# A transformer layer on one core: wider weight blocks in one feed-forward stage, and another spacing of the modulation rows

## The chip, the core and the metric

The kernel runs on one core of a Trainium2 chip. The metric is the device time of one execution in microseconds (us). Lower is better. The time of the kernel before is the median of 3 runs, 1873.0 us.

The engines are named as in the profile: PE (matrix products; PEld is its weight load, which overlaps them), DVE (vector operations), ACT (activations and casts), POOL, and SP, which here only issues DMAs.

## What is computed

One layer over 256 rows of 2048 numbers, in float32. Nine modulation vectors of 2048 numbers come from a conditioning vector `c`. They shift, scale and gate three sub-layers: feed-forward, token mixer (attention and a recurrent part), feed-forward.

```python
ada = (silu(c) @ w_ada + b_ada)            # 2048 x 18432 weights, one vector in
sh1, sc1, g1, sh2, sc2, g2, sh3, sc3, g3 = split(ada, 9)
h = swiglu(layernorm(x) * (1 + sc1) + sh1, ffn1_w_in, ffn1_w_out)
x = layernorm(ALPHA * x + 0.5 * (1 + g1) * h, ln1_g, ln1_b)
h = token_mixer(layernorm(x) * (1 + sc2) + sh2, w_in, ..., w_out)
x = layernorm(ALPHA * x + (1 + g2) * h, ln2_g, ln2_b)
h = swiglu(layernorm(x) * (1 + sc3) + sh3, ffn2_w_in, ffn2_w_out)
x = layernorm(ALPHA * x + 0.5 * (1 + g3) * h, ln3_g, ln3_b)
# swiglu(h) = (silu(h @ w_gate) * (h @ w_up)) @ w_out, with 5632 hidden columns
```

## The kernel before, in words

**Products.** Each float32 operand is split into a high part and a rest (`hi`, `lo`), and a product is three matmuls of these parts (`mm3`, L420 to L422). A weight block of 1 MB is loaded by SP into one of three places called `raw` (`load_w`). It is then split in two halves: ACT casts `hi` (L155), DVE subtracts to get `lo` (L156). `hi` and `lo` have six places each, so the split can run up to three blocks ahead of PE.

**Stages, in order.** First input, first part (`first_in`, tiles `s`, `raw_s`): half of the first feed-forward's hidden columns, while the first modulation vectors are made. First input, second part (`ffn_in` with tag `f1`, tiles `gu_f`, `raw_f1i`, from about 311 to 526.5 us): the other hidden columns, `j` from 12 to 21. First output (`out_proj` with tag `f1`, `raw_f1o`, to about 757 us). A layer norm (`boundary`). The mixer (783 to 1159 us): `cols_1024`, `cols_form_b`, `form_a_four`, then `out_proj` with tag `mx`. A second layer norm, and the second feed-forward to the end.

**The second part of the first input.** For each `j` and each of gate and up (`gu`), 256 columns are computed from two blocks of 1024 inputs by 256 columns. One PSUM tile of 512 columns holds gate and up of one group of 128 hidden columns. After both, ACT takes the Silu of gate and DVE multiplies (L459, L460).

**The ada rows.** The modulation vectors are not made by PE but by DVE, beside the products. A unit is 1024 columns of `w_ada` over 2048 inputs, in 16 rows of 128 inputs. A row (called an ada row below) is a 512 KB load by SP into one of two places `araw` (L189; `ar` in the profile) and one multiply-add on DVE into an accumulator `acc` or `gate` (L170). After 16 rows a tail splits the sum (`alo`), sums it over partitions on PE (`bc`, L183), and spreads it (`dg`, `scsh`, or into `gate`, L200 to L215).

**What sets their order.** `AdaQueue` holds the units in order. After each weight block a stage calls `pump(rate)`. This adds the rate to a debt, does one step of a pending tail, and issues whole rows while the debt is at least 1. The rates are one line of constants (`R_F`, `R_IN`, `R_OUT`, `R_MX`, ...). A unit of the first stage can't start before the layer norm that follows it allows it (`stage`), and a unit with its own accumulator waits for pending tails that have one. `need(n)` forces what is missing before a point of use, and drops the debt. `finish1` needs 6 units (96 rows) before the first layer norm; the mixer's output needs 10 units.

**Queues.** SP issues its loads in program order and stops at one whose place is still in use. DVE, ACT and PE run in order too. So an ada row whose load is late holds up everything behind it on DVE.

**The mixer's recurrent heads.** For head `h`, PE makes `gb` and `sps` (L1426, L1428), ACT an exponential of `gb`, and DVE multiplies them into `dm` (L1433, L1434). `sps` has one place (`fifth_tile`), so the `sps` of head 1 waits until DVE has read that of head 0.

Of the kernel before, what the change touches and what calls it, by code (L numbers as in the profile page):

```python
# [9 lines left out]
AF = mybir.ActivationFunctionType  # L10
ALU = mybir.AluOpType
# [3 lines left out]
P = 128  # L15
T = 256
D = 2048
KD = D // P
DFF = 5632
# [13 lines left out]
def layer_kernel(  # L33
# [8 lines left out]
    V, S, G_, PE, SP = nc.vector, nc.scalar, nc.gpsimd, nc.tensor, nc.sync  # L42
# [101 lines left out]
    pin = {}  # L144
# [9 lines left out]
    def split(src, hi, lo):  # L154
        S.copy(hi, src)  # L155
        return V.tensor_tensor(out=lo, in0=src, in1=hi.bitcast(F32), op=ALU.subtract)  # L156
# [62 lines left out]
    class AdaQueue:  # L219
# [42 lines left out]
        def pump(self, n):  # L262
            self.owed += n
            self.end_step()
            while self.owed >= 1:
                with pinned():
                    if not self.row():
                        break
                self.owed -= 1
# [104 lines left out]
    def new_xT(tag):  # L374
        x = xp.tile([P, KD, 2, T], F32R, name=f"x_{tag}")
        return x[:, :, 0], x[:, :, 1], x


    def load_w(src, nk, w, name, by_parts=False, behind=None, into=None):
        raw = wp.tile([P, nk, w], F32, tag="raw", bufs=3, name=f"raw_{name}")  # L380
        src = src.rearrange("(k p) n -> p k n", p=P)
        if not by_parts:
            SP.dma_start(raw, src)
        h = nk // 2 if nk * w <= 2048 else nk // 4
        for q in range(nk // h):
            if by_parts:
                SP.dma_start(raw[:, q * h:(q + 1) * h], src[:, q * h:(q + 1) * h])
            if into:
                hi, los = into[q]
                S.copy(hi, raw[:, q * h:(q + 1) * h, :])  # L390
                n = h // len(los)
                for i, lo in enumerate(los):
                    pin["w"] = V.tensor_tensor(out=lo, in0=raw[:, q * h + i * n:q * h + (i + 1) * n, :],
                                               in1=hi[:, i * n:(i + 1) * n, :].bitcast(F32), op=ALU.subtract).ins
                for kk in range(h):
                    yield q * h + kk, hi[:, kk, :], los[kk // n][:, kk % n, :]
                continue
            hi = wp.tile([P, h, w], F32R, tag="hi", bufs=6, name=f"hi_{name}{q}")
            lo = wp.tile([P, h, w], F32R, tag="lo", bufs=6, name=f"lo_{name}{q}")
            with ExitStack() as s:  # L400
                if behind:
                    s.enter_context(tc.issue_after(behind))
                pin["w"] = split(raw[:, q * h:(q + 1) * h, :], hi, lo).ins
            for kk in range(h):
                yield q * h + kk, hi[:, kk, :], lo[:, kk, :]

    def woven(b):
        if b.shape[-1] % 256:
            return b
        return b.rearrange("p (a n) -> p n a", a=2)  # L410

    def unwoven(ps):
        return ps.rearrange("p (n a) -> p a n", a=2)

    def halves(v):
        return v.rearrange("p (a n) -> p a n", a=2)

    def mm3(o, ah, al, bh, bl, start, stop):
        bh, bl = woven(bh), woven(bl)
        PE.matmul(o, ah, bh, start=start, stop=False)  # L420
        PE.matmul(o, ah, bl, start=False, stop=False)  # L421
        PE.matmul(o, al, bh, start=False, stop=stop)  # L422

    def mm2(o, ah, al, x, start, stop):
        PE.matmul(o, ah, x.rearrange("p s (a n) -> p s n a", a=2), start=start, stop=False)  # L425
        PE.matmul(o[:, T:], al, woven(x[:, 0]), start=False, stop=stop)  # L426


    def cols_form_a(src, c0, outs, xT, name, npump, khs=(0, 1)):
        xhi, xlo, x = xT  # L430
        for kh in khs:
            for k8, hi, lo in load_w(src[kh * 1024:(kh + 1) * 1024, c0:c0 + 256], 8, 256, f"{name}_{kh}"):
                k = kh * 8 + k8
                for f in range(2):
                    fs = slice(f * P, (f + 1) * P)
                    start, stop = k == 8 * khs[0], k == 8 * khs[-1] + 7
                    if outs[f].shape[-1] == 2 * T:
                        mm2(outs[f], hi[:, fs], lo[:, fs], x[:, k], start, stop)
                    else:
                        mm3(outs[f], hi[:, fs], lo[:, fs], xhi[:, k, :], xlo[:, k, :], start, stop)  # L440
            npump()

    def ffn_in(w, xT, hT, j0, tag, npump, values=None):
        def one(j, gu, outs):
            last = gu and j == DFF // 256 - 1
            cols_form_a(w, gu * DFF + j * 256, outs, xT, f"{tag}i{j}_{gu}", (lambda: None) if last else npump)

        def both(dst, ps):
            S.copy(dst, unwoven(ps[:, :T]))
            V.tensor_tensor(out=dst, in0=dst, in1=unwoven(ps[:, T:]), op=ALU.add)  # L450

        for j in range(j0, DFF // 256):
            if values is None:
                ps = [mm_tile(f"gu_{tag}{j}_{f}") for f in range(2)]
                for gu in range(2):
                    one(j, gu, [p[:, gu * T:(gu + 1) * T] for p in ps])
                for f in range(2):
                    h = halves(hT[:, 2 * j + f, :])
                    S.activation(h, unwoven(ps[f][:, :T]), AF.Silu)  # L459
                    pin["h"] = V.tensor_tensor(out=h, in0=h, in1=unwoven(ps[f][:, T:]), op=ALU.mult).ins  # L460
                continue
            for gu in range(2):
                ps = [mm_tile(f"gu_{tag}{j}_{gu}{f}") for f in range(2)]
                one(j, gu, ps)
                for f in range(2):
                    h = halves(hT[:, 2 * j + f, :])
                    if gu:
                        u = halves(values.tile([P, T], F32, tag="u", bufs=2, name=f"u_{tag}{j}_{f}"))
                        both(u, ps[f])
                        pin["h"] = V.tensor_tensor(out=h, in0=h, in1=u, op=ALU.mult).ins  # L470
                    else:
                        both(h, ps[f])
                        S.activation(h, h, AF.Silu)
        for _ in range(2):
            npump()

# [311 lines left out]
    def entry_of(load, got, u0, u1):  # L788
        for u in range(u0, u1):
            got[u] = []  # L790
            for item in load(u):
                got[u].append(item)
                yield

    R_F, R_IN, R_OUT, R_MX, R_A, R_B = 1.25, 1.2, 1, 1.42, 1.05, .6
    NP = 2
    right = dict(side="right")
    def at(rate):  # L800
        return lambda: pump(rate)
# [18 lines left out]
    hT = Rows(hp, "hT1")  # L820
# [3 lines left out]
    xT = new_xT("f1")  # L824
    W1 = ffn1_w_in[0]
# [127 lines left out]
    NS = 12  # L953
# [99 lines left out]
    def first_hi_places(tag):  # L1053
        ent["hi0"] = tc.alloc_tile_pool(name=f"hi0{tag}", bufs=1)
        ent["hi"] = [ent["hi0"].tile([P, 2, T], F32R, name=f"hi{tag}_{k}") for k in range(0, 8, 2)]

    first_hi_places("1")
    ffn_in(W1, xT, hT, NS, "f1", at(R_IN))
    xp.release()
    need(2)  # L1060
    W = w_in[0]
# [76 lines left out]
    xhi, xlo, _ = xT  # L1138
# [377 lines left out]
    for i, c0 in enumerate((C_MQ, C_MK)):  # L1516
        ps = form_a_four(c0, f"m{i}")
# [76 lines left out]
    xT = new_xT("f2")  # L1594
# [13 lines left out]
    hT = Rows(hp, "hT2")  # L1608
# [23 lines left out]
    for j in range(2, 10):  # L1632
# [18 lines left out]
    for j in range(2, 10):  # L1651
        for gu, ps in enumerate(half_in(j, 1, "fs")):
# [7 lines left out]
            for f in range(2):  # L1660
                i = 2 * j + f
                h = hT[:, i + 16 * gu, :]
# [55 lines left out]
```

## Time and profile before

| what | value |
|---|---|
| median of 3 runs | 1873.0 us (1867.44 to 1874.89) |
| profiled execution, its own time | 1878.46 us |
| span of the profiled execution | 1876.8 us |
| granted TensorE clock, mean | 0.996 |
| DMA moved | 510.74 MB, mean 272 GB/s |

The span runs from the first to the last instruction; 1.7 us of the profiled execution's own time lie around it. In the views, a row of windows gives for a stretch of time the busy time of each engine with its instruction count, then the granted clock, the mean busy share of the 16 DMA engines and the rate in GB/s. A row of waits names who waited, for whom, how long in total, how often, and the longest. A row of the timeline has start, length, engine, line, operation and tiles, and in square brackets the idle time before it and what ended it.

### The profile page before, as it was taken

The numbers are of one execution on the slowest core, as the hardware profiler recorded it, in microseconds if no ns is written. First come the engines' busy times: TensorE is split into PE (matmuls) and PEld (weight loads), VectorE is DVE, ScalarE is ACT, GpSimd is POOL, SyncE is SP. The second block draws the span as 40 slices with busy tenths as digits, with TensorE's granted clock in tenths as the row PEclk, the third lists the DMA queues.
The fourth block names the chain that finished last, engine by engine and source line by source line (L and its number), as shares of the span: only waits on it lengthen the run. The fifth ranks groups of instructions, "written<-read, shape, count | busy, mean of one in ns | idle before, by whom it ended". The sixth has DMA issues, their size and how long they took to land.

```text
span 1876.8 us, 29775 instructions
## 1 busy us (share of the span) xinstructions
PE 1829.0 (97%) x11881; PEld 1673.8 (89%) x11881; DVE 1465.0 (78%) x1883; ACT 911.8 (49%) x1320; POOL 62.2 (3%) x92
## 2 busy tenths in 40 slices
PE   7999999999999999999989999999999999999997
PEld 5999999999998888699989887888999999988887
DVE  6888989778788886878879788988977766574655
ACT  3554363443454433845556545565444454554441
POOL 1211200000000000100000000000000000000000
PEclk9999999999999999999999999999999999999999
DMA  9988978999998898489978894998878776666664
GB/s 365 383 279 294 333 232 274 313 312 325 296 315 305 309 329 296 136 301 331 316 254 307 303 314 142 307 305 265 271 253 265 260 241 193 201 202 204 205 204 146
DMA packets 283906, 510.74 MB, mean 272 GB/s; under 512 B 10834, under 2 KB 134386, under 8 KB 282744
## 3 DMA queue, kind: packets, MB, share of 16 engines
q1 hardware_dynamic: 275656, 477.90, 75.0%
q0 software_dynamic: 8112, 30.95, 4.8%
q8 instruction: 93, 1.52, 0.3%
q14 instruction: 45, 0.37, 0.1%
HBM read 506.71 MB, written 2.10 MB: 271 GB/s over the span
## 4 chain that ended last, share of the span: by engine, by line
PE 38%; DMA 10%; DVE 8%; issue 2%; ACT 2%; POOL 0%; DVEq 0%; ACTq 0%; SPq 0%; POOLq 0%
PE gu_f L425 9%; DMA ar<-in_w_ada_dram 7%; PE gu_f L426 4%; PE o_f L421 4%; PE o_f L420 4%; PE o_f L422 4%; PE fs L425 3%; DMA raw_fh<-in_ffn_w_in_dram 2%; DVE acc L170 2%; PE fs L426 1%; DVE gate L170 1%; PE fh L425 1%; PE b_mv L421 1%; PE b_mv L420 1%; PE b_mv L422 1%
## 5 line engine op out<-in xcount | busy, mean ns | idle before, releaser
L170 DVE SCALAR_TENSOR_TENSOR acc<-ar,csil,acc 128x1024 f32<-128x1024 f32 (+1 forms) x167 | 211.7, 1269 | 74.3 <-DMA ar<-in_w_ada_dram 73.7
L425 PE MATMUL gu_f<-x_f,hi_f2i 128*128 128x512 f32 x768 | 251.8, 382 | 0.0
L422 PE MATMUL s<-x_f,lo_s 128*128 128x256 f32 x768 | 211.9, 276 | 0.8 <-DVE lo_s L156 0.7
L420 PE MATMUL s<-x_f,hi_s 128*128 128x256 f32 x768 | 212.2, 277 | 0.2 <-ACT x_f L336 0.2
L421 PE MATMUL s<-x_f,hi_s 128*128 128x256 f32 x768 | 212.0, 276 | 0.0
L426 PE MATMUL gu_f<-x_f,lo_f2i 128*128 128x256 f32 x768 | 209.3, 273 | 0.0
L422 PE MATMUL gu_f<-x_f,lo_f1i 128*128 128x256 f32 x640 | 176.4, 276 | 1.4 <-DVE lo_f1i L156 1.3
L421 PE MATMUL gu_f<-x_f,hi_f1i 128*128 128x256 f32 x640 | 176.0, 275 | 0.0
L420 PE MATMUL gu_f<-x_f,hi_f1i 128*128 128x256 f32 x640 | 176.0, 275 | 0.0
L156 DVE TENSOR_TENSOR lo_f2o<-raw_f2o,hi_f2o 128x1024 fp32r<-128x1024 f32 x86 | 105.2, 1225 | 86.9 <-ACT hi_f2o L155 86.8
L156 DVE TENSOR_TENSOR lo_f2i<-raw_f2i,hi_f2i 128x1024 fp32r<-128x1024 f32 x96 | 117.5, 1224 | 65.7 <-ACT hi_f2i L155 64.8
L425 PEld LDWEIGHTS gu_f<-x_f,hi_f2i 128*128 128x128 f32 x768 | 145.1, 189 | 20.3
L155 ACT CAST hi_s<-raw_s 128x1024 fp32r<-128x1024 f32 x96 | 99.5, 1051 | 128.7 <-PE s L421 77.0
L422 PEld LDWEIGHTS s<-x_f,lo_s 128*128 128x128 f32 x768 | 147.9, 193 | 1.2 <-DVE lo_s L156 1.2
L421 PEld LDWEIGHTS s<-x_f,hi_s 128*128 128x128 f32 x768 | 147.9, 193 | 0.4 <-DVE x_f L339 0.4
L420 PEld LDWEIGHTS s<-x_f,hi_s 128*128 128x128 f32 x768 | 147.8, 193 | 0.3 <-ACT x_f L336 0.3
L426 PEld LDWEIGHTS gu_f<-x_f,lo_f2i 128*128 128x128 f32 x768 | 147.4, 192 | 0.2
L155 ACT CAST hi_f2o<-raw_f2o 128x1024 fp32r<-128x1024 f32 x86 | 90.0, 1047 | 115.7 <-PE o_f L422 107.5
L155 ACT CAST hi_f2i<-raw_f2i 128x1024 fp32r<-128x1024 f32 x96 | 100.4, 1045 | 91.3 <-PE gu_f L425 65.3
L155 ACT CAST hi_f1o<-raw_f1o 128x1024 fp32r<-128x1024 f32 x86 | 88.5, 1047 | 113.7 <-DMA raw_f1o<-in_ffn_w_out_dram 55.0
L170 DVE SCALAR_TENSOR_TENSOR gate<-ar,csil,gate 128x1024 f32<-128x1024 f32 (+1 forms) x94 | 117.6, 1252 | 29.0 <-DMA ar<-in_w_ada_dram 28.9
L155 ACT CAST hi_f1i<-raw_f1i 128x1024 fp32r<-128x1024 f32 x80 | 81.3, 1049 | 111.6 <-DMA raw_f1i<-in_ffn_w_in_dram 80.2
(449 smaller groups left out, 5095.4 us busy)
## 6 DMA issues: line engine op xcount, KB each, us to landing
ar<-in_w_ada_dram SPq DMA_DIRECT2D x230, 512.0 KB, 5.5
raw_f2i<-in_ffn_w_in_dram SPq DMA_DIRECT2D x48, 1024.0 KB, 5.2
raw_s<-in_ffn_w_in_dram SPq DMA_DIRECT2D x47, 1024.0 KB, 7.6
raw_f1o<-in_ffn_w_out_dram SPq DMA_DIRECT2D x44, 1024.0 KB, 7.3
raw_f2o<-in_ffn_w_out_dram SPq DMA_DIRECT2D x44, 1024.0 KB, 5.2
raw_f1i<-in_ffn_w_in_dram SPq DMA_DIRECT2D x40, 1024.0 KB, 7.8
ar<-in_w_ada_dram POOLq DMA_DIRECT2D x45, 512.0 KB, 6.4
raw_mxo<-in_w_out_dram SPq DMA_DIRECT2D x16, 1024.0 KB, 7.7
```

The source lines that it names most:

```text
L155: S.copy(hi, src)
L156: return V.tensor_tensor(out=lo, in0=src, in1=hi.bitcast(F32), op=ALU.subtract)
L170: V.scalar_tensor_tensor(out=acc, in0=raw, scalar=csil[:, k:k + 1], in1=acc, op0=ALU.mult, op1=ALU.add)
L420: PE.matmul(o, ah, bh, start=start, stop=False)
L421: PE.matmul(o, ah, bl, start=False, stop=False)
L422: PE.matmul(o, al, bh, start=False, stop=stop)
L425: PE.matmul(o, ah, x.rearrange("p s (a n) -> p s n a", a=2), start=start, stop=False)
L426: PE.matmul(o[:, T:], al, woven(x[:, 0]), start=False, stop=stop)
```

## The change

The second part of the first input gets a function of its own. It takes 512 columns at a time, in blocks of 512 inputs by 512 columns, again 1 MB each: each row of a block is now 2 KB in one piece where it was 1 KB. For each 512 columns it runs four blocks of gate and then four of up. One PSUM tile now holds two groups of 128 columns of gate, or two of up. The Silus of four groups follow each other after the gate blocks, and four multiplies after the up blocks. There are 40 blocks before and after, 1920 matmuls of the same shape, 20 Silus and 20 multiplies of the same shape, and 40 calls of `pump` (two blocks at the end call none, two calls stand behind). The old branch without `values` goes.

Two rates change: `R_IN` from 1.2 to 1.3, `R_MX` from 1.42 to 1.3.

```diff
+    def ffn_in_512(w, xT, hT, q0, tag, npump):
+        xhi, xlo, _ = xT
+        for q in range(q0, DFF // 512):
+            for gu in range(2):
+                ps = [mm_tile(f"gu_{tag}{q}_{gu}{i}") for i in range(2)]
+                for u in range(4):
+                    c0 = gu * DFF + q * 512
+                    for k4, hi, lo in load_w(w[u * 512:(u + 1) * 512, c0:c0 + 512], 4, 512, f"{tag}i{q}_{gu}{u}"):
+                        k = 4 * u + k4
+                        for f in range(4):
+                            fs = slice(f * P, (f + 1) * P)
+                            mm3(ps[f // 2][:, f % 2 * T:(f % 2 + 1) * T], hi[:, fs], lo[:, fs], xhi[:, k, :], xlo[:, k, :],
+                                k + f % 2 == 0, k + f % 2 == KD)
+                    if not (gu and q == DFF // 512 - 1 and u > 1):
+                        npump()
+                for f in range(4):
+                    h, p = halves(hT[:, 4 * q + f, :]), unwoven(ps[f // 2][:, f % 2 * T:(f % 2 + 1) * T])
+                    if gu:
+                        pin["h"] = V.tensor_tensor(out=h, in0=h, in1=p, op=ALU.mult).ins
+                    else:
+                        S.activation(h, p, AF.Silu)
...
-    R_F, R_IN, R_OUT, R_MX, R_A, R_B = 1.25, 1.2, 1, 1.42, 1.05, .6
+    R_F, R_IN, R_OUT, R_MX, R_A, R_B = 1.25, 1.3, 1, 1.3, 1.05, .6
...
-    ffn_in(W1, xT, hT, NS, "f1", at(R_IN))
+    ffn_in_512(W1, xT, hT, NS // 2, "f1", at(R_IN))
```

The rates move ada rows against everything else. In names such as `ar6_0_4`, the first two numbers are the unit and the last is its row, 0 to 15; the number behind is a buffer's.

On SP, at the end of the first output: `raw_f1o1536_5` to `_10` are the last weight blocks of that product, and `raw_mo0` is the first of the mixer. Before:

```order
L383 DMA raw_f1o1536_5_7823<-in_ffn1_w_out_dram 128x4x512
L189 DMA ar6_0_0_8427<-in_w_ada_dram 128x2x512
L383 DMA raw_f1o1536_6_7857<-in_ffn1_w_out_dram 128x4x512
L189 DMA ar6_0_1_8454<-in_w_ada_dram 128x2x512
L383 DMA raw_f1o1536_7_7919<-in_ffn1_w_out_dram 128x4x512
L383 DMA raw_f1o1536_8_7927<-in_ffn1_w_out_dram 128x4x512
L383 DMA raw_f1o1536_9_7944<-in_ffn1_w_out_dram 128x4x512
L383 DMA raw_f1o1536_10_7954<-in_ffn1_w_out_dram 128x4x512
L1066 DMA raw_mo0_8070<-in_w_in_dram 128x2x1024
```

The same place on SP with the change:

```order
L383 DMA raw_f1o1536_8_7956<-in_ffn1_w_out_dram 128x4x512
L189 DMA ar6_0_2_7847<-in_w_ada_dram 128x2x512
L189 DMA ar6_0_3_7850<-in_w_ada_dram 128x2x512
L383 DMA raw_f1o1536_9_7966<-in_ffn1_w_out_dram 128x4x512
L189 DMA ar6_0_4_7853<-in_w_ada_dram 128x2x512
L189 DMA ar6_0_5_7890<-in_w_ada_dram 128x2x512
L383 DMA raw_f1o1536_10_7976<-in_ffn1_w_out_dram 128x4x512
L189 DMA ar6_0_6_7927<-in_w_ada_dram 128x2x512
L1078 DMA raw_mo0_8092<-in_w_in_dram 128x2x1024
```

Before, two rows of unit 6_0 are loaded ahead of the layer norm and none is added up there. With the change rows 0 to 8 of it are loaded and rows 0 to 6 are added up ahead of the layer norm, five of their loads between or behind the last three weight blocks.

On DVE, in the mixer, between the last splits of the block group `fb` and the multiplication of head 0 (`dm0`, which frees `sps0`). Before:

```order
L156 TENSOR_TENSOR lo_fb30_10221<-raw_fb3_10218,hi_fb30_10220 128x1024
L156 TENSOR_TENSOR lo_fb31_10249<-raw_fb3_10218,hi_fb31_10248 128x1024
L170 SCALAR_TENSOR_TENSOR acc5_0_9893<-ar5_0_7_10276,csil_94,acc5_0_9893 128x1024
L170 SCALAR_TENSOR_TENSOR acc5_0_9893<-ar5_0_8_10279,csil_94,acc5_0_9893 128x1024
L200 TENSOR_TENSOR dg6_1_1_10187<-bc6_1_1_10184,ident_79 128x512
L202 TENSOR_REDUCE scsh_103<-dg6_1_1_10187 128x4
L204 TENSOR_TENSOR scsh_103<-scsh_103,bcol_98 128x2x4
L1433 TENSOR_TENSOR dm0_10206<-dm0_10206,trir_87 128x128 x2
L1434 TENSOR_TENSOR dm0_10206<-sps0_10205,dm0_10206 128x256
```

The same place on DVE with the change:

```order
L156 TENSOR_TENSOR lo_fb30_10233<-raw_fb3_10230,hi_fb30_10232 128x1024
L156 TENSOR_TENSOR lo_fb31_10261<-raw_fb3_10230,hi_fb31_10260 128x1024
L170 SCALAR_TENSOR_TENSOR acc5_0_9622<-ar5_0_11_10288,csil_94,acc5_0_9622 128x1024
L1445 TENSOR_TENSOR dm0_10218<-dm0_10218,trir_87 128x128 x2
L1446 TENSOR_TENSOR dm0_10218<-sps0_10217,dm0_10218 128x256
```

One ada row stands ahead of `dm0` where two and the end of a tail stood.

On SP, the loads of these rows among the weight blocks `fb` and `fbk`. Before:

```order
L383 DMA raw_fb3_10218<-in_w_in_dram 128x4x512
L189 DMA ar5_0_6_10191<-in_w_ada_dram 128x1024
L189 DMA ar5_0_7_10276<-in_w_ada_dram 128x1024
L383 DMA raw_fbk0_10298<-in_w_in_dram 128x4x512
L383 DMA raw_fbk1_10390<-in_w_in_dram 128x4x512
L189 DMA ar5_0_8_10279<-in_w_ada_dram 128x1024
```

With the change:

```order
L383 DMA raw_fb3_10230<-in_w_in_dram 128x4x512
L189 DMA ar5_0_9_10134<-in_w_ada_dram 128x1024
L189 DMA ar5_0_10_10203<-in_w_ada_dram 128x1024
L383 DMA raw_fbk0_10307<-in_w_in_dram 128x4x512
L189 DMA ar5_0_11_10288<-in_w_ada_dram 128x1024
L383 DMA raw_fbk1_10402<-in_w_in_dram 128x4x512
```

The last row ahead of `dm0` was behind both blocks `fbk0` and `fbk1` (row 8); it is now behind `fbk0` alone (row 11).

More of the change, by code (lines that the diff above doesn't have):

```diff
@@ L441, in cols_form_a, with ffn_in @@
             npump()
[L443 to L446, printed above, removed]
+    def ffn_in(w, xT, hT, j0, tag, npump, values):
         def both(dst, ps):
@@ L452, in ffn_in @@
         for j in range(j0, DFF // 256):
[L453 to L461, printed above, removed]
             for gu in range(2):
                 ps = [mm_tile(f"gu_{tag}{j}_{gu}{f}") for f in range(2)]
-                one(j, gu, ps)
+                last = gu and j == DFF // 256 - 1
+                cols_form_a(w, gu * DFF + j * 256, ps, xT, f"{tag}i{j}_{gu}", (lambda: None) if last else npump)
                 for f in range(2):
@@ L473, in ffn_in @@
                         S.activation(h, h, AF.Silu)
+        for _ in range(2):
+            npump()
[13 more added lines that the diff above has]
+                    if not (gu and q == DFF // 512 - 1 and u > 1):
+                        npump()
+                for f in range(4):
[4 more added lines that the diff above has]
+                        S.activation(h, p, AF.Silu)
         for _ in range(2):
```

## Prediction

> **What bounds the kernel now.** I read the page first, then the windows by stage, then PE's waits inside the stages that the change touches.
>
> ```profile
> span 1876.8 us, 29775 instructions
> PE 1829.0 (97%) x11881; PEld 1673.8 (89%) x11881; DVE 1465.0 (78%) x1883; ACT 911.8 (49%) x1320; POOL 62.2 (3%) x92
> ```
>
> PE is busy for 1829.0 of 1876.8 us. A change that leaves PE's work alone can only remove idle time, 47.8 us in all, or slow matmuls behind it. The windows show where that idle time lies (columns: length, busy PE, PEld, DVE, ACT, POOL, clock, DMA share, GB/s).
>
> ```profile
> core 0: us, PE busy (x) PEld busy (x) DVE busy (x) ACT busy (x) POOL busy (x), PEclk, DMA share, GB/s
> 311.00:526.50 215.50, 214.09 (x1897) 212.81 (x1896) 166.34 (x170) 89.22 (x108) 1.08 (x2) 1.00 0.94 310
> 526.50:757.00 230.50, 230.50 (x1068) 201.13 (x1067) 189.13 (x209) 102.00 (x119) 2.59 (x3) 1.00 0.86 301
> 783.00:1159.00 376.00, 361.42 (x2438) 335.41 (x2436) 314.28 (x471) 205.03 (x372) 9.30 (x13) 1.00 0.85 293
> ```
>
> The stage that gets the new code (311 to 526.5) has 215.50 - 214.09 = 1.4 us of idle PE, the first output behind it none, the mixer 376.00 - 361.42 = 14.6 us. So the new block shape can win at most 1.4 us where it stands. What can be won lies in the mixer, where the change only moves ada rows. PE's waits there:
>
> ```profile
> PE sps L1428 <- DVE dm L1434: 5.0, 1, 5.0
> PE o_mx L422 <- DVE ylo L156: 2.9, 1, 2.9
> PE o_mx L420 <- ACT yF L1251: 2.1, 1, 2.1
> PE pr_fb L422 <- DVE lo_fb L156: 1.5, 1, 1.5
> PE b_fv L421 <- DVE lo_fv L156: 1.0, 1, 1.0
> PE b_mv L421 <- DVE lo_mv L156: 0.8, 1, 0.8
> ```
>
> Nearly all end with DVE, and one is 5.0 us long. DVE's timeline just before its end tells why:
>
> ```profile
> 943.31 0.69 DVE L156 TENSOR_TENSOR alo<-gate,ahi 128x512 fp32r<-128x512 f32 x1
> 943.91 2.36 DVE L156 TENSOR_TENSOR lo_fb<-raw_fb,hi_fb 128x1024 fp32r<-128x1024 f32 x2
> 946.19 1.28 DVE L170 SCALAR_TENSOR_TENSOR acc<-ar,csil,acc 128x1024 f32<-128x1024 f32 x1
> 952.17 1.28 DVE L170 SCALAR_TENSOR_TENSOR acc<-ar,csil,acc 128x1024 f32<-128x1024 f32 x1 [4.71 <-DMA ar<-in_w_ada_dram]
> 953.38 0.68 DVE L200 TENSOR_TENSOR dg<-bc,ident 128x512 f32<-128x512 f32 x1
> 954.10 0.69 DVE L202 TENSOR_REDUCE scsh<-dg 128x4 f32<-128x512 f32 x1
> 954.82 0.17 DVE L204 TENSOR_TENSOR scsh<-scsh,bcol 128x8 f32<-128x8 f32 x1
> 954.90 0.49 DVE L1433 TENSOR_TENSOR dm<-dm,trir 128x128 f32<-128x128 f32 x2
> 955.30 0.42 DVE L1434 TENSOR_TENSOR dm<-sps,dm 128x256 f32<-128x256 f32 x1
> ```
>
> DVE stands 4.71 us for the load of an ada row (row 8 of unit 5_0). Behind it in order are a tail's last steps (1.5 us) and `dm0`, which frees the only place of `sps`. SP shows why the row is late:
>
> ```profile
> 935.93 5.10 SPq L383 DMA_DIRECT2D raw_fbk<-in_w_in_dram  x2
> 943.43 0.34 SPq L189 DMA_DIRECT2D ar<-in_w_ada_dram  x1
> ```
>
> Its load is issued at 943.43, behind two 1 MB blocks and behind DVE's earlier rows, and DVE has it at 952.17, 8.7 us later. After the wait the clock is low too:
>
> ```profile
> 955.80:963.00 7.20, 7.20 (x49) 7.02 (x50) 7.20 (x11) 3.40 (x7) 0.00 (x0) 0.78 0.59 206
> ```
>
> At a granted 0.78 over 7.20 us PE loses 0.22 x 7.20 = 1.6 us more.
>
> **The change part by part.** *Matmuls, Silus, multiplies, splits:* the same count and shapes; 0.
>
> ```profile
> L460 DVE TENSOR_TENSOR hT<-hT,gu_f 128x256 f32<-128x256 f32 x18 | 7.4, 415 | 0.0
> ```
>
> The only order that differs is four Silus or four multiplies in a row. They wait in PSUM tiles that PE needs again a block and a half later or more (five tiles in turn, two per 21 us); at the end of the stage the fourth tile of the first output needs the first two multiplies, 2 x 0.415 = 0.8 us of DVE, while PE fills three others for 9 x 0.22 = 2.0 us (the pitch below). Cost 0, up to 1 us if an ada row stands ahead of them.
>
> *Rows of 2 KB instead of 1 KB, and 4 more ada rows in the stage.* 40 calls at 1.3 instead of 1.2 are 52 rows instead of 48, so the stage must load 40 x 1.049 + 52 x 0.524 = 69.2 MB in 215.5 us, or 321 GB/s, where 310 were moved at a busy share of 0.94. Whether that fits:
>
> ```profile
> 40.00:160.00 120.00, 118.51 (x1057) 117.94 (x1056) 100.26 (x103) 64.30 (x83) 21.86 (x30) 1.00 0.92 332
> 315.00:520.00 205.00, 203.59 (x1803) 202.31 (x1802) 156.80 (x160) 86.01 (x102) 1.08 (x2) 1.00 0.94 310
> ```
>
> The first window is the first part of the same input, whose blocks have 2 KB rows already: 332 / 0.92 = 361 GB/s at a full share. The second has the 1 KB rows: 310 / 0.94 = 330. 321 is 0.89 of the first and 0.97 of the second; both fit, so PE stays fed. I take the first, as it is the same load. The Trainium skill (DMA: Bandwidth & Descriptors, Specifications) gives 512 B as the smallest transfer at line rate. By it 2 KB rows bring nothing over 1 KB, the share would be 0.97, and the sum would still be 0; the two rows above differ by 9%, which speaks against it. DVE gets 4 x 1.28 = 5.1 us more on 166.34 of 215.50: hidden. Value 0, bounds -1.4 (all idle time gone) and the rival below.
>
> *The first output and the layer norm.* Before, 9 x 1.25 + 48 + 40 = 99 rows were due, but the 3 beyond unit 3_3 were refused while its tail was pending, and the debt was dropped: 96 were done. Now 103 are due, the tail is done earlier, and 7 rows of unit 6_0 are added up before the layer norm. They fall on the end of the first output:
>
> ```profile
> 715.00:738.30 23.30, 23.30 (x109) 20.13 (x108) 13.78 (x15) 11.54 (x12) 1.06 (x2) 1.00 0.83 299
> 736.99 1.23 DVE L156 TENSOR_TENSOR lo_f1o<-raw_f1o,hi_f1o 128x1024 fp32r<-128x1024 f32 x1
> 747.54 0.70 DVE L538 TENSOR_TENSOR o_f<-o_f,gate 128x512 f32<-128x512 f32 x1 [5.73 <-PE o_f L422]
> ```
>
> The last split ends at 738.2. PE finishes the first half of the last four blocks at 747.5; that half is 48 matmuls at 230.5 / 1068 = 0.216 us, 10.4 us, so the fourth block is needed at about 744.9. Slack 6.7 us. Added ahead of it: 7 rows and 2.2 us of tail steps, 11.2 us, against 23.30 - 13.78 = 9.5 us in which DVE was idle. If all of that is usable the split is 1.7 us later, if none 11.2. Value 0, bounds 0 and 11.2 - 6.7 = 4.5 us.
>
> *The mixer.* 57 calls: 80 rows at 1.42 (to the stage's limit), 73 at 1.3.
>
> ```profile
> 783.00:1159.00 376.00, 0.00 (x0) 0.00 (x0) 99.83 (x80) 0.00 (x0) 1.00 0.85 293
> ```
>
> This is the window of the ada loads' tiles alone: 80 rows, 99.83 us of DVE, 1.25 each. 7 fewer free 8.7 us of DVE and 3.7 MB of loads, 12.5 us at 293 GB/s. Most of that is idle time saved elsewhere; what counts is each wait of PE. For `sps`: one row (11) stands ahead of `dm0` instead of two and a tail. Its place is freed by row 9, which now precedes the convolution's block of DVE work, and it is issued behind `fbk0` only, which went out at 935.93. At the 8.7 us of row 8 it lands near 945, before DVE's splits end at 946.3. Then `dm0` is done near 946.3 + 1.3 + 1.2 = 948.8, before PE comes at 950.8. So the 5.0 us go, and with them the 1.6 us of low clock: -6.6. Next late there is `lo_fb`: up to that split DVE has three rows less (3.8 us) but the tail of 6_1 more (0.7 for `alo` and 1.4 and 1.5 for its two spreads, 3.6 us), so its 1.5 us stay. The other waits sit at the same places with the same or one row fewer ahead of them. I keep them: 0, bounds -5 (half of the other 9.6) and +3 (one new wait of the size of `ylo`'s).
>
> *Later stages.* One row of unit 6_3 moves by a block: 0.
>
> Sum: 0 + 0 + 0 - 6.6 = -6.6 us, 1878.5 to 1871.9 us for a profiled execution. The runs' median is 1873.0, 5.5 below that one execution, within the spread of 1867.4 to 1874.9; I take the difference from the median: **1866.4 us**.
>
> **The rivals.** *(1) The wait comes back.* DVE's work up to `dm0` falls by only four rows, about 5 us, and PE gains on it; if row 11 or another load lands as late as row 8 did, PE waits there or one block later. For it: DVE is busy 314.28 of 376.00 us and four of the six waits above end with a split on DVE. Against: the loads' demand falls too. Then 1873.
>
> *(2) The other waits go too.* 7 rows fewer let the splits run ahead; half of the other 9.6 us go: 1866.4 - 5 = 1861.4. Against: `yF` and `ylo` sit late in the mixer, where the rows stand at about the same places again.
>
> *(3) Slower: the rows' own chain in the second part.* There are two places for row loads, so two rows take at least one landing and a multiply-add.
>
> ```profile
> L189 SPq DMA_DIRECT2D ar<-in_w_ada_dram x46: 327/367/1746, 313.6 to 523.2; - x46
> DMA to landing us min/median/max: 3.9/5.0/8.6
> ```
>
> SP stops behind a row without a place, and the weight blocks with it. A block takes 215.5 / 40 = 5.39 us. At 1.3 rows per block the chain decides above 2 x 5.39 / 1.3 = 8.3 us for two rows. That 1.2 went unhindered shows at most 2 x 5.39 / 1.2 = 9.0. At 9.0 the cost is 40 x (0.65 x 8.98 - 5.39) = 17.9 us: 1884.3; midway 1875. Against: the median is 5.0 + 1.3 = 6.3.
>
> **How the numbers follow.** Forecast 0.52, rival 1 0.20, rival 2 0.17, rival 3 0.11. The measurement can tell about 0.5%, 9.4 us: below 1863.6 (faster) or above 1882.4 (slower). Faster: rival 2 and the forecast's lower edge, 0.20. Slower: the upper third of rival 3 and an end of the first output that costs more than its bound, 0.07. Same 0.73. The range takes the forecast from 1862 to 1871 (its bounds of +4.5 and -5), rival 1 with the runs' spread of some 4 us, rival 2 down to nine tenths of the other 9.6 us, and rival 3 to its middle and 3 us of spread: **1858 to 1878**.
>
> **What would show it.** Right: between 311 and 757 PE idles no more than 2 us, with a DMA share near 0.9 and 52 rows in the input's second part; no wait of PE for `dm` over 1 us, and the clock at 1.00 through the mixer; 73 rows from 783 to 1159; `ylo`'s and `yF`'s waits still there. Wrong: PE waiting for `lo_f1i` block after block (rival 3); PE waiting for `lo_f1o` in the last 20 us before the layer norm; a wait over 3 us elsewhere in the mixer (rival 1); `ylo` and `yF` under 1 us each (rival 2).

## The result and the profile after

| | before | after |
|---|---|---|
| median | 1872.8 us (20 runs, 1866.4 to 1882.5) | 1881.4 us (20 runs, 1875.5 to 1888.4) |
| ratio | | **1.0041** (95% interval 1.0026 to 1.0056) |
| profiled execution: its own time, span | 1878.46, 1876.8 us | 1888.39, 1886.7 us |

The change made the kernel slower by 0.41%, 7.7 us (the medians alone lie 8.6 us apart; the ratios are used throughout). The forecast was 6.6 us the other way, and its range ended at 1878. The two profiled executions differ by 9.9 us. Both lie above their medians (by 5.6 and 7.0 us), so single microseconds of a stage are read from the profiles, but what a change is worth is read from the ratios.

The windows of after, at the stage borders of PE (columns as in the prediction):

```profile
core 0: us, PE busy (x) PEld busy (x) DVE busy (x) ACT busy (x) POOL busy (x), PEclk, DMA share, GB/s
305.50:536.50 231.00, 220.86 (x1935) 218.68 (x1934) 172.49 (x174) 90.23 (x111) 1.08 (x2) 0.99 0.88 300
536.50:771.50 235.00, 231.99 (x1070) 201.20 (x1068) 195.24 (x216) 102.72 (x118) 2.96 (x4) 1.00 0.87 305
797.00:1170.30 373.30, 362.30 (x2437) 336.73 (x2436) 307.37 (x463) 205.39 (x371) 8.71 (x13) 0.99 0.83 285
```

The second part of the first input takes 231.0 us where it took 219.7 (from 307.0 to 526.7). The first output takes 3.9 us more. The mixer is shorter, as forecast, but by 376.00 - 373.30 = 2.7 us only (2.4 between the same two instructions). In the second part PE idles 231.00 - 220.86 = 10.1 us, and the DMA engines are *less* busy than before: 0.88 at 300 GB/s, not 0.94 at 310. So it is not a full DMA that holds PE up. PE's waits in that stage of after:

```profile
PE gu_f L422 <- DVE lo_f1i L156: 6.8, 6, 2.3
PE bc L183 <- DVE alo L156: 3.3, 1, 3.3
```

This is the sign that the prediction named for its third rival: PE waits for `lo_f1i`, and for `alo`, which stands in DVE's order too. But it does not wait "block after block". The stage of after in three parts:

```profile
305.50:400.00 94.50, 91.67 (x809) 90.73 (x808) 73.22 (x74) 36.77 (x47) 0.00 (x0) 1.00 0.90 308
400.00:440.00 40.00, 32.69 (x268) 31.62 (x267) 26.29 (x28) 13.62 (x17) 1.08 (x2) 0.96 0.84 275
440.00:536.50 96.50, 96.50 (x862) 96.33 (x862) 72.98 (x73) 39.85 (x47) 0.00 (x0) 1.00 0.88 303
```

Of the 10.1 us, 7.3 lie between 400 and 440, and none behind 440, though the rows go on at the same rate. In these 40 us a gate unit ends: its two `alo` stand on DVE at 408 and 431, and PE's wait of 3.3 us is for the second. What DVE does before one of PE's waits there (DVE's timeline of after):

```profile
405.72 1.23 DVE L156 TENSOR_TENSOR lo_f1i<-raw_f1i,hi_f1i 128x1024 fp32r<-128x1024 f32 x1 [4.86 <-ACT hi_f1i L155]
406.87 1.40 DVE L483 TENSOR_TENSOR hT<-hT,gu_f 128x256 f32<-128x256 f32 x4
408.19 0.69 DVE L156 TENSOR_TENSOR alo<-gate,ahi 128x512 fp32r<-128x512 f32 x1
408.79 0.75 DVE L168 TENSOR_SCALAR acc<-ar,csil 128x1024 f32<-128x1024 f32 x1
409.46 1.21 DVE L156 TENSOR_TENSOR lo_f1i<-raw_f1i,hi_f1i 128x1024 fp32r<-128x1024 f32 x1
410.59 1.27 DVE L170 SCALAR_TENSOR_TENSOR acc<-ar,csil,acc 128x1024 f32<-128x1024 f32 x1
411.79 1.21 DVE L156 TENSOR_TENSOR lo_f1i<-raw_f1i,hi_f1i 128x1024 fp32r<-128x1024 f32 x1
416.63 1.28 DVE L170 SCALAR_TENSOR_TENSOR acc<-ar,csil,acc 128x1024 f32<-128x1024 f32 x1 [3.63 <-DMA ar<-in_w_ada_dram]
417.84 2.35 DVE L156 TENSOR_TENSOR lo_f1i<-raw_f1i,hi_f1i 128x1024 fp32r<-128x1024 f32 x2
```

And SP's timeline of after for the same rows:

```profile
391.69 3.30 SPq L189 DMA_DIRECT2D ar<-in_w_ada_dram  x2
395.09 6.17 SPq L383 DMA_DIRECT2D raw_f1i<-in_ffn_w_in_dram  x3
409.57 0.37 SPq L189 DMA_DIRECT2D ar<-in_w_ada_dram  x1
410.70 0.37 SPq L383 DMA_DIRECT2D raw_f1i<-in_ffn_w_in_dram  x1
411.89 6.42 SPq L189 DMA_DIRECT2D ar<-in_w_ada_dram  x2
```

Two rows are issued from 391.69 on. DVE uses the first at 408.79, since a split whose block came late stands ahead of it (4.86 us idle). Only then is a place free, and SP issues the next row at 409.57, the next block behind it. DVE stands for that row until 416.63, with the next splits behind it. In this stretch a late block makes a row late, and the late row makes the next splits late.

In the mixer the wait for `sps` is gone, as forecast. PE's waits there in after:

```profile
PE pr_fb L422 <- DVE lo_fb L156: 3.2, 1, 3.2
PE ptp L1320 <- DVE gate L215: 2.9, 1, 2.9
PE o_mx L420 <- DVE res L552: 2.1, 1, 2.1
PE b_mv L421 <- DVE lo_mv L156: 1.2, 1, 1.2
```

### The profile page after: what moved, and what is told of

It reads as the page before. It is cut to its first block, busy times and chain, and to the rows that moved or that the text cites. A ratio compares the mean times of both kernels' runs of the same rounds, so it can differ in the third digit from the quotient of the medians.

```text
span 1886.7 us, 29769 instructions
## 1 busy us (share of the span) xinstructions
PE 1832.9 (97%) x11881; PEld 1675.6 (89%) x11881; DVE 1467.3 (78%) x1883; ACT 912.1 (48%) x1320; POOL 61.7 (3%) x92
## 4 chain that ended last, share of the span: by engine, by line
PE 40%; DMA 8%; DVE 7%; issue 2%; ACT 2%; POOL 0%; SPq 0%; DVEq 0%; ACTq 0%; POOLq 0%
PE gu_f L425 9%; DMA ar<-in_w_ada_dram 5%; PE gu_f L426 4%; PE o_f L422 4%; PE o_f L420 4%; PE o_f L421 4%; PE fs L425 3%; DMA raw_fh<-in_ffn_w_in_dram 2%; PE fs L426 1%; PE o_mx L420 1%; PE o_mx L421 1%; PE o_mx L422 1%; DVE gate L170 1%; DMA raw_m<-in_w_in_dram 1%; DVE acc L170 1%
```

## The experiments

"Places" are the places `araw` for row loads. Ratios are against the kernel before, run beside it on the same chip, with the 95% interval. 0.1% is 1.9 us. The last columns are from one profiled execution each: the length of the first input's second part (219.7 us before, 231.0 after), and how long DVE stood for rows there.

| | blocks | rates (input, mixer) | places | ratio | interval | stage, us | DVE for rows, us |
|---|---|---|---|---|---|---|---|
| before | 256 | 1.2, 1.42 | 2 | 1 | | 219.7 | 33.6 |
| after | 512 | 1.3, 1.3 | 2 | 1.0041 | 1.0026 to 1.0056 | 231.0 | 34.5 |
| e1 | 256 | 1.3, 1.42 | 2 | 1.0082 | 1.0060 to 1.0104 | 224.5 | 37.4 |
| e2 | 512 | 1.2, 1.3 | 2 | 0.9985 | 0.9969 to 1.0001 | 221.0 | 27.0 |
| e3 | 256 | 1.2, 1.3 | 2 | 0.9978 | 0.9958 to 0.9997 | 218.5 | 30.7 |
| e4 | 512 | 1.3, 1.3 | 3 | 0.9978 | 0.9956 to 1.0001 | 219.0 | 9.5 |
| e12 = e4 | 512 | 1.3, 1.3 | 3 | 0.9993 | 0.9973 to 1.0013 | 221.6 | 6.6 |
| e5 | 256 | 1.3, 1.3 | 3 | 1.0005 | 0.9984 to 1.0027 | 218.9 | 11.9 |
| e6, rows on POOL's queue | 512 | 1.3, 1.3 | 2 | 1.0084 | 1.0054 to 1.0114 | 231.9 | 56.0 |
| e7 | 512 | 1.4, 1.25 | 3 | 0.9996 | 0.9971 to 1.0021 | 219.8 | 4.1 |
| e8 | 256 | 1.2, 1.42 | 3 | 1.0021 | 0.9999 to 1.0043 | 222.7 | 9.0 |
| e9 | 256 | 1.3, 1.3 | 2 | 1.0025 | 1.0009 to 1.0042 | 225.0 | 36.1 |
| e10 | 512 | 1.4, 1.25 | 2 | 1.0088 | 1.0060 to 1.0116 | 230.5 | 29.5 |
| e11 | 512 | 1.2, 1.3 | 3 | 1.0014 | 0.9993 to 1.0035 | 223.0 | 4.6 |
| e13, 8 multiply-adds more | 256 | 1.2, 1.3 | 2 | 1.0023 | 1.0006 to 1.0040 | 219.7 | 28.2 |
| e14 | 512 | 1.3, 1.3 | 3, late | 0.9986 | 0.9966 to 1.0005 | 217.6 | 7.6 |
| e15 | 256 | 1.3, 1.3 | 3, late | 0.9986 | 0.9969 to 1.0004 | 218.0 | 12.2 |
| e16, 8 loads more | 256 | 1.2, 1.3 | 2 | 1.0045 | 1.0026 to 1.0064 | 227.5 | 34.4 |

Differences of two ratios below are worked out from this table; their bounds are the root of the two half-intervals' squares.

The last column tells two places (27 to 56 us) from three (4 to 12), but not the kernels that lose from those that don't: before and e3 have 33.6 and 30.7, after and e10 34.5 and 29.5. What tells them apart is PE between 400 and 440 us. With two places and 1.3 or 1.4 it idles 3.6 (e9), 4.4 (e1), 7.3 (after) and 7.0 us (e10) there, and 3.3 in e6; in each of e9, e1 and e10 most of that is one wait for the gate's `alo` (2.8, 3.2, 6.1 us). With two places and 1.2 it idles 0.3 us (before), 0.0 (e3) and 1.1 (e2), and with more work put in 0.5 (e13) and 2.0 (e16). With three places it idles 0.0 in all eight profiles, whatever the rate and the blocks. Here e9, then e5, the same kernel with three places:

```profile
400.00:440.00 40.00, 36.41 (x303) 35.77 (x304) 30.16 (x33) 18.27 (x22) 1.08 (x2) 0.96 1.00 329
400.00:440.00 40.00, 40.00 (x356) 39.83 (x356) 32.65 (x35) 16.26 (x19) 1.07 (x2) 1.00 1.02 338
```

### The parts one by one (e1, e2, e3, e9)

Theory A: the rows' chain through two places is what got slow, because of the rate. Theory B: the wide block form itself got slow. The edits, on the line of rates of before (e1, e3, e9) and of after (e2):

```diff
-    R_F, R_IN, R_OUT, R_MX, R_A, R_B = 1.25, 1.2, 1, 1.42, 1.05, .6
+    R_F, R_IN, R_OUT, R_MX, R_A, R_B = 1.25, 1.3, 1, 1.42, 1.05, .6   # e1
+    R_F, R_IN, R_OUT, R_MX, R_A, R_B = 1.25, 1.2, 1, 1.3, 1.05, .6    # e3
+    R_F, R_IN, R_OUT, R_MX, R_A, R_B = 1.25, 1.3, 1, 1.3, 1.05, .6    # e9
...
-    R_F, R_IN, R_OUT, R_MX, R_A, R_B = 1.25, 1.3, 1, 1.3, 1.05, .6
+    R_F, R_IN, R_OUT, R_MX, R_A, R_B = 1.25, 1.2, 1, 1.3, 1.05, .6    # e2
```

e1: 

> The kernel before with one number changed: 1.3 ada rows per block in the first input's second part instead of 1.2. Blocks of 256 columns and the mixer's 1.42 stay. Theory A (the rows' chain through two places is what got slow, because of the rate): the second part takes about 230 us instead of 219.7, PE waits for lo_f1i and alo there, and the time is about 1881 us (ratio near 1.005). Theory B (the wide block form itself got slow: bursts of four Silus and four multiplies, another order of SP and DVE): the second part stays near 220 us and the time near 1873 (ratio 1.000), since the mixer keeps its wait for dm.

e2: 

> The changed kernel with one number put back: 1.2 ada rows per block in the first input's second part; wide blocks and the mixer's 1.3 stay. Theory A: the second part is back at about 220 us, and with the mixer's wait for dm gone the time is about 1866 us (ratio 0.9965). Theory B: the second part stays at 228 us or more and the time near 1880 (ratio 1.004).

e3: 

> The kernel before with one number changed: 1.3 rows per block in the mixer instead of 1.42. Nothing is changed ahead of the mixer. If the mixer's part of the prediction holds by itself, the 5.0 us wait for dm and the 1.6 us of low clock go and the time is about 1866.4 us (ratio 0.9965), with up to 3 us of other waits. If the gain came only from the rows that the first input's second part took over, the wait is still there and the time is 1873 (ratio 1.000).

e9: 

> The changed kernel with the blocks of 256 columns put back: both rates at 1.3, two places. It takes the wide form alone out. If two places give a row every 4.4 to 4.6 us whatever the blocks are (theory A), 52 rows still take 225 to 231 us, the mixer's wait for dm is gone as with wide blocks, and the time is within 5 us of the changed kernel (ratio 1.002 to 1.006). If the wide form made the loss (theory B), the second part is near 220 us and the ratio 0.998.

With old blocks the rate costs too: e1 1.0082, and e9, which has the mixer's new rate as well, 1.0025. (e1 costs more than theory A asked. In its profile some 11 us of that are lost as late as the stage `fh` behind the mixer, which takes 100.3 us instead of 89.0, with 24 rows added up in it instead of 18; why so many fall there stays open.) The rate put back takes the loss away: e2 0.9985. With these the change splits into three steps: the mixer's rate (before to e3) -0.22%, -4.1 us (-7.9 to -0.6); the wide blocks (e3 to e2) +0.07 (± 0.25)%, nothing that shows, though up to 0.3% isn't excluded; the input's rate (e2 to after) +0.56 (± 0.22)%, **+10.5 us**. With blocks of 256 columns the last step (e3 to e9) is +0.47 (± 0.26)%, +8.8 us, and after against e9 is +0.16 (± 0.22)%. Theory B falls as the cause of the loss. In the profiles the step e3 to e9 is 6.5 us longer, e2 to after 10.0 us, and of these 10.0 some 1.7 us are a low clock behind the 3.3 us wait for `alo` (0.24 x 7.00; window of after):

```profile
431.00:438.00 7.00, 6.08 (x40) 5.98 (x41) 6.67 (x7) 2.00 (x2) 0.54 (x1) 0.76 0.84 272
```

One thing stays open: at 1.3 with two places the stage is 6.0 us longer with wide blocks than with old ones (231.0 against 225.0), but the times differ by 3.0 us only (± 4.1).

e3 also tests the mixer's term by itself. The wait for `sps` is gone there, but another came on the next product: PE stands for `gb` behind a tail's step on DVE (PE's waits of e3 in the mixer):

```profile
PE gb L1426 <- DVE dg L200: 3.7, 1, 3.7
PE pr_fb L422 <- DVE lo_fb L156: 2.4, 1, 2.4
```

### A third place for the rows (e4, e5, e12, e8, e11)

The edit: during the first input's second part every third row goes to a place of its own. e4 and e12 are after with it, e5 is e9 with it, e8 before with it, e11 e2 with it.

```diff
+    third = []
     def ada_rows(acc, src, tag):
         for k in range(KD):
-            raw = ap.tile(list(acc.shape), F32, tag="araw", bufs=2, name=f"ar{tag}_{k}")
+            if third and k % 3 == 2:
+                raw = third[0].tile(list(acc.shape), F32, tag="ax", name=f"ar{tag}_{k}")
+            else:
+                raw = ap.tile(list(acc.shape), F32, tag="araw", bufs=2, name=f"ar{tag}_{k}")
...
+    third.append(tc.alloc_tile_pool(name="ax", bufs=1, **right))
     ffn_in_512(W1, xT, hT, NS // 2, "f1", at(R_IN))
+    third.pop().release()
```

e4: 

> The changed kernel, with a third place for the ada rows' loads during the first input's second part (every third row goes there); rates 1.3 and 1.3, wide blocks. Theory A, in the form that SP stops behind a row without a place and the weight blocks with it: the waits of PE for lo_f1i and alo mostly go, the second part falls from 231 to about 221 us, and the time from 1881 to about 1871 (ratio 0.999). Theory B (bursts on DVE and ACT, or the order): the second part stays above 228 us and the time near 1880 (ratio 1.004).

e12, the same kernel beside others: 

> The kernel with wide blocks, three places and the rates 1.3 and 1.3 once more, beside the other three on one chip, to bring its distance to the kernel before (0.9978, 0.9956 to 1.0001) to within 0.15% and to set it beside the run at 1.2: theory A says 0.9965 to 0.999.

e5: 

> The kernel before with blocks of 256 columns, both new rates (1.3 and 1.3) and a third place for the ada rows' loads in the first input's second part. If places alone decide (theory A), the second part takes 219 to 221 us, as with wide blocks and three places, and the time is about 1871 us (ratio 0.998): the wide blocks bring nothing. If 1 KB rows run out of DMA time at 1.3 (321 of the 330 GB/s worked out from the profile before), the second part takes 223 us or more, with a DMA share over 0.95, and the time is 1875 or more.

The stage of e4, and DVE's waits in it:

```profile
306.40:525.40 219.00, 217.30 (x1933) 216.60 (x1932) 173.43 (x174) 91.74 (x110) 1.07 (x2) 1.00 0.91 321
```

```profile
DVE lo_f1i L156 <- ACT hi_f1i L155: 28.5, 26, 2.7
DVE acc L170 <- DMA ar<-in_w_ada_dram: 8.7, 8, 2.3
...
DVE gate L170 <- DMA ar<-in_w_ada_dram: 0.8, 2, 0.6
```

The same rows and blocks as in after, now in 219.0 us, at 321 GB/s and a share of 0.91: just the rate that the prediction asked of the DMA. DVE stands for rows 9.5 us instead of 34.5. The mean of e4 and e12 is 0.56 (± 0.21)% below after, 10.4 us, the whole price of the rate with wide blocks. With old blocks the stage shortens to the same length in the profile (218.9 us, from 225.0), but the time of e5 against e9 is only -0.20 (± 0.27)%: not shown there.

e8: 

> The kernel before with the third place alone (1.2, 1.42, blocks of 256 columns). The second part has 1.4 us of idle PE to lose, the mixer keeps its rate and its wait for dm: 1872 to 1873 us (ratio 0.999 to 1.000) by every theory. If it is faster by over 3 us, the third place does something else than to free the rows' chain at the higher rate, and the reading of the run with three places falls.

e11: 

> Wide blocks, three places, 1.2 rows per block in the second part and 1.3 in the mixer: a candidate for the best version. With 1.2 the rows' chain was not yet in the way, so by theory A the third place adds nothing here: second part 219 to 220 us, mixer without the wait for dm, ratio 0.997 to 0.999. If three places also take away delays that two places cause at 1.2 already, it is under 0.997.

At 1.2 the third place brings nothing and rather costs: +0.21 (± 0.22)% (e8 against before) and +0.29 (± 0.26)% (e11 against e2). SP's timeline of e8 at the start of the stage shows why it might:

```profile
311.00 6.14 SPq L194 DMA_DIRECT2D ar<-in_w_ada_dram  x3
321.04 0.38 SPq L388 DMA_DIRECT2D raw_f1i<-in_ffn_w_in_dram  x1
```

Three rows go ahead of a weight block. Before, two did, from 309.71, and the block went out at 315.48. PE's wait of e8 for the split behind it, in all the stage (1.3 us before):

```profile
PE gu_f L427 <- DVE lo_f1i L156: 3.7, 1, 3.7
```

### Who is held up by the late row (e6)

The edit: `(G_ if own else SP).dma_start(raw, ...)` at L189, with `own` set during the stage, so POOL issues the rows there.

> The changed kernel with two places, its ada rows of the first input's second part issued by POOL's queue instead of SP's. Theory A1 (SP, stopped behind a row without a place, keeps the weight blocks back): SP has no row in its queue, so the waits for lo_f1i mostly go, the second part is near 220 us and the time near 1871 (ratio 0.998). Theory A2 (DVE stands for a late row in front of the splits, whoever issues it): two places still give each row its turn late, the second part stays at 227 us or more, the time at 1878 or more (ratio over 1.002).

It was 1.0084, with 231.9 us in the stage. SP's and DVE's waits of e6 there:

```profile
SPq L385 <- DVE lo_f1i L156: 174.4, 34, 12.5
```

```profile
DVE acc L170 <- DMA ar<-in_w_ada_dram: 39.0, 20, 5.9
DVE gate L170 <- DMA ar<-in_w_ada_dram: 14.0, 8, 4.9
DVE lo_f1i L156 <- ACT hi_f1i L155: 6.9, 7, 1.6
```

No row stands in SP's way, and SP is ahead: it waits 174.4 us for DVE to empty the weight places. Yet the stage is as long as in after. So theory A1 can't be the whole, and A2 held: DVE stands for late rows in front of the splits (56.0 us) even where SP is free. The loss is not the same one throughout: one wait of 4.7 us for `lo_f1i` at the start of the stage is new in e6, while the wait for the gate's `alo` is there as in after (2.8 us). What SP's standing adds in after is thus not shown. The Trainium skill (Trainium Kernel Development and Optimization, Key Constraints) says that DMAs of all issuing queues share the same 16 engines, and that issuing from several saves issue time alone; this run agrees: the rows' median from issue to landing was 5.7 us in both after and e6.

### The dose (e7, e10)

The edit: the rates 1.4 and 1.25, in e4 (e7) and in after (e10).

e7: 

> The changed kernel with three places, 1.4 rows per block in the second part and 1.25 in the mixer. Theory A with places as the only limit: 1.4 rows per block are 3.85 us per row, 11.6 us for three, above the 8.9 us that a place was occupied on average in the kernel before; so the second part stays near 220 us and the time near 1870 (ratio 0.997 to 0.998). If the DMA's time is the next limit (about 326 GB/s wanted where 320 ran at a share of 0.91), the second part is 222 to 226 us and the time 1873 to 1877.

e10: 

> The changed kernel with two places, 1.4 rows per block in the second part and 1.25 in the mixer: the run at 1.4 with three places, without the third place. Theory A in numbers: two places gave a row every 4.43 to 4.67 us in all the runs so far, so the 55 rows that took 219.8 us with three places take 55 x 4.5 = 248 us (240 to 255), PE waits for lo_f1i over and over, and the time is 25 to 30 us above the run with three places (ratio 1.011 to 1.017). If the 11 us at 1.3 were an accident of one order of instructions, not a limit per row, the second part stays below 235 us.

With three places the stage holds 1.4 at 219.8 us and 327 GB/s, a share of 0.92. With two the kernel is 0.92 (± 0.38)% slower than that, some 17 us; against the 0.56 (± 0.21)% at 1.3 that is more by 0.36 (± 0.43)%, so a growth with the rate isn't shown. And the number for the stage was wrong: it took 230.5 us, not 248, and so stayed below the 235 that was named for the other reading, an accident of one order. A fixed time per row through two places is not the law. Against an accident of one order stand the five orders that lose with two places (after, e1, e9, e10, e6) and the same stretch without idle PE in all with three. What fits both is a pile-up at one place of the order, the end of the gate unit, which needs late rows to form. A part of e10's loss comes later, where the multiplies on DVE are late and hold the first output's PSUM tile (PE's waits of e10 from 304 to 781 us; the wait for `alo` is that of the gate):

```profile
PE o_f L420 <- DVE hT L483: 6.6, 1, 6.6
PE bc L183 <- DVE alo L156: 6.1, 1, 6.1
```

### DVE's time or the load (e13, e16), and the third place later (e14, e15)

e13 and e16 are e3 with more work in the stage, at 8 of its 40 blocks:

```diff
+            V.scalar_tensor_tensor(out=more, in0=more, scalar=csil[:, 0:1], in1=more, op0=ALU.mult, op1=ALU.add)   # e13
...
+            SP.dma_start(more, w_ada[0, (calls[0] // 5) * P:(calls[0] // 5 + 1) * P, :1024])   # e16
+            V.tensor_scalar_mul(one, more[:, :1], csil[:, 0:1])
```

e13: 

> The kernel before with 1.3 in the mixer (0.9978 by itself) and, in the first input's second part, 8 more multiply-adds on DVE of an ada row's shape, on a tile that is there already, so without a load; their result is not used. Theory D (DVE has no free time there: its idle time is 33.6 us of waits for rows and 15.8 for casts that stand in its order): 8 x 1.28 = 10.2 us more, ratio 1.002 to 1.004. Theory L (a row costs by its late load, DVE's time is free): below 2 us more, ratio 0.997 to 0.999.

e16: 

> The kernel before with 1.3 in the mixer and, in the first input's second part, 8 more loads of an ada row's size into a place of their own, spaced like the multiply-adds of the run with more DVE work; DVE reads one column of each (0.1 us), and nothing uses them. Theory L in the form that the loads take the DMA's time from weight blocks and rows (326 GB/s wanted, 330 worked out as full): 5 us or more, ratio 1.000 to 1.003. Theory D: below 3 us, ratio 0.997 to 0.9995.

Neither half of a row is free. Against e3, the multiply-adds alone cost +0.45 (± 0.26)%, 8.4 us, the loads alone +0.67 (± 0.27)%, 12.5 us. (In e16's trace DVE's reads take 0.2 us each, and DVE never waits for one.) Divided by 8 and added that is 1.05 + 1.56 = 2.6 us per row, if the two halves add; the four rows of the change, at 8.8 to 10.5 us, cost 2.2 to 2.6 each. But the intervals are wide, and the profile shows the price of the loads in the stage (227.5 us against 218.5), but that of the multiply-adds not: e13's stage takes 219.7 us, 1.2 more than e3's, and its first output starts with a 3.2 us wait for a multiply. That DVE has no time left with two places is thus only half shown. With three it has: e7's stage holds 179.5 us of DVE work in 219.8 us, that of before 169.2 in 219.7.

e14 and e15 open the third place from the fourth `pump` on, in after and in e9.

e14: 

> The changed kernel (wide, 1.3, 1.3) with the third place open only from the fourth block on, so that the order of SP at the start of the stage is that with two places. If the third place's price lies in those first blocks, PE's wait for lo_f1i at 314 to 320 us is under 1.5 us, the second part takes 217 to 219 us and the ratio is 0.996 to 0.998. If not, it is as before, 0.998 to 1.000.

e15: 

> The same with blocks of 256 columns (1.3, 1.3, third place from the fourth block on). With two places this was 1.0025, with three from the start 1.0005. If the loss at 1.3 is the late rows, whatever the blocks, and the third place's own price is at the start: 0.996 to 0.998. If old blocks lose at 1.3 for another reason than late rows: 1.000 to 1.003.

PE's wait at the start of the stage is gone in both. The stage takes 217.6 and 218.0 us, the shortest here; for e14:

```profile
306.90:524.50 217.60, 217.60 (x1933) 216.66 (x1932) 172.91 (x174) 90.30 (x110) 1.08 (x2) 1.00 0.91 323
```

Both kernels have 0.9986: with old blocks the late third place takes 0.39 (± 0.24)% off e9's time, which e5 had not shown; with wide ones it adds nothing to e4's. Neither ratio came in the 0.996 to 0.998 that was expected if the third place's own price lay at the start, though e14's stage did; that this price lies there is thus seen in the profiles, not in the times. With three places, wide and old blocks are alike at 1.3 too. Of all the versions e3 alone lies below the kernel before with its whole interval, and only just: the mixer's rate changed, nothing else. e2, e14, e15 and the mean of e4 and e12 are within 0.1% of it.

## Why the prediction was wrong

**Matmuls, Silus, multiplies in another order: 0.** Right within what shows: wide against old blocks +0.07% at 1.2, +0.16% at 1.3, both within their bounds. The first output does wait for the multiplies, 1.6 us where up to 1 was allowed. But the wide form isn't needed for that: e1, e5, e13 and e15, with old blocks, wait 1.8 to 3.2 us there.

**2 KB rows and 4 more ada rows: 0. This is the step that failed.** It said that 321 GB/s fit, "so PE stays fed", and of DVE's 5.1 us on 166.34 of 215.50: "hidden". The step cost 10.5 us. Both averages were right as averages: with three places the DMA moved 321 GB/s at 0.91. With two places the rows came late to DVE all the same, and where the gate unit ends the splits and `alo` behind them came late to PE. What the 5.1 us were set against is in DVE's waits of before from 311 to 526.5 us:

```profile
DVE acc L170 <- DMA ar<-in_w_ada_dram: 18.0, 11, 3.9
DVE lo_f1i L156 <- ACT hi_f1i L155: 15.8, 7, 4.4
DVE gate L170 <- DMA ar<-in_w_ada_dram: 10.7, 6, 4.9
DVE acc L168 <- DMA ar<-in_w_ada_dram: 3.1, 1, 3.1
```

DVE's idle time there was 31.8 us for rows and 15.8 for casts of late blocks: 47.6 of the 49.2 that 215.50 - 166.34 leaves. So it was not free time in DVE's order: DVE stood for loads in it, and a row more brings its own load to stand for. It becomes usable where the loads come in time, as e7 shows. And SP's waits of before for a place, over the whole stage:

```profile
SPq L189 <- DVE acc L170: 43.5, 27, 3.5
...
SPq L189 <- DVE gate L170: 20.8, 15, 1.9
```

42 times, in a stage with 48 rows, SP waited for DVE to free a place: the places were nearly always in use at 1.2 already. This view alone is no sign of a loss, though. In e4, where PE idles 1.7 us in all the stage, SP still waits 45 times for 52 rows (77.4 us). PE is hit only where the splits' lead of up to three blocks is used up. Why that happens at the gate unit's end at 1.3 and not at 1.2 was followed in one stretch of one trace, and is beyond that argued.

**The rival that came nearest.** The third rival named the two places and the sign. It was given 0.11 because a row's turn was put at 5.0 + 1.3 = 6.3 us, landing and multiply-add, below the 8.3 at which it decides. That left out how long a landed row waits for its turn on DVE: rows issued from 391.69 on were used from 408.79 on, 17 us later. Of the 17.9 us that it priced at most, 10.5 came, but that doesn't confirm its sum. Its law, a fixed time for two rows in every block, failed at 1.4, PE lost its time in one stretch, and SP need not stop behind a row for the loss (e6).

**The first output and the layer norm: 0, bounds 0 and 4.5.** In the profile 3.9 us more. That this is within the bounds is luck: the prediction put the cost at the end, under the added rows, and there, in the last 20 us before the layer norm, PE waits 0.3 us. 1.6 us are the wait for the multiplies at the start, 1.1 short waits for `lo_f1o` before 650 us. PE's waits of after in the first output:

```profile
PE o_f L420 <- DVE hT L483: 1.6, 1, 1.6
PE o_f L421 <- DVE lo_f1o L156: 1.4, 3, 0.9
```

**The mixer: -6.6, bounds -5 and +3.** The rows were as forecast: 73, and no wait for `dm`. By itself (e3) the rate brings -4.1 us (-7.9 to -0.6): right in mechanism and sign, with a wait of 3.7 us for `gb` in return, which is the first rival's "one block later". In after the mixer is only 2.7 us shorter in the profile: `pr_fb` waits 3.2 us instead of 1.5, `ptp` 2.9 instead of 0, and the clock was not 1.00 but 0.99, while the waits for `ylo` and `yF` went and one of 2.1 us for `res` came. With blocks of 256 columns at 1.3 in the input (e1 to e9) the same edit brings -0.57 (± 0.28)%, -10.7 us, and most of that isn't the mixer's: of the 19.3 us between the two profiles 12.2 lie in `fh` behind it, where e1 adds up 24 rows and e9 17. What a rate gains depends on the order that the other stages leave, and is not one number.

## What to carry to other kernels

An engine's idle time is room for more work only if nothing in its own order uses it up: before work is called hidden, split the idle time by what ended it, and take off the waits that the new work lengthens. Two streams that fit by their averages (loads and vector work) can still hold each other up through too few places; how long a place is held is read from issue to last use, not from landing plus one operation. That places are always in use, or that an engine often stands for loads, doesn't yet say that they cost time: look where the bounding engine idles, and compare that stretch with one place more. Here a third place took the loss away at the higher rates; at the lower one it gained nothing and may have cost 0.2 to 0.3%.

## What was not expected of the hardware

- Rows of 2 KB take less of the DMA engines' time than rows of 1 KB: 309 GB/s at a share of 0.90 (e2) against 313 at 0.95 (e3), and 323 at 0.91 (e14) against 321 at 0.96 (e15). Per GB/s that is 4 to 6% less, and none of it shows in the time (0.9985 and 0.9978; 0.9986 both). The Trainium skill (DMA: Bandwidth & Descriptors, Specifications) puts line rate at transfers of 512 B and more; the times agree, the shares do not quite.
- One profiled execution can mislead by more than the effect: e5's was the fastest of its 12 runs (1867.5 us at a median of 1877.4).
